# The lower half of the tokens in two parts of 256, and gathered expert steps moved between stages

## The chip, the cores and the metric

The kernel runs on one core of one Trainium2 chip. The metric is the device time of one execution in microseconds (us). Before the change three runs took 3245.26, 3264.1 and 3249.8 us, median 3249.8 us.

## What is computed

One layer of a decoder over 1024 tokens of width 1024 in float32:

```python
h = rms_norm(x, norm_mix_g); proj = h @ w_in          # 28 blocks of 128 columns and the gates
da_out = diff_attention(...)                           # 4 heads, causal, ALiBi
ml_out = rms_norm(o_gate * mlstm_chunkwise(...))       # 4 heads, state carried over the tokens
x = x + concat(da_out, ml_out) @ w_out
x = x + peer_ffn(rms_norm(x, norm_ffn_g), ...)         # expert retrieval
gate = sigmoid(rms_norm(x, norm_ple_g) @ w_ple_gate)
x = x + gate * (p @ w_ple_proj); out = rms_norm(x, final_norm_g)

def peer_ffn(x):                                       # per token
    q = x @ w_query                                    # 8 heads x 2 halves of 128
    sv, si = top_k(q . sub_keys, 16)                   # per half, of 128 keys
    top_s, eidx = top_k(all sums of two halves, 16)    # 16 of 16384 experts per head
    a = gelu(x . expert_u[eidx])
    return sum(softmax(top_s) * a * expert_v[eidx])    # 128 experts per token
```

## The kernel before

Tokens lie in eight tiles of 128. `front(part, ptk)` (L220) takes a part of `T` = 512 tokens (`NT` = 4 tiles) through the mixer, the output projection and the queries; it is called for part 0 (tiles 0 to 3) and part 1 (tiles 4 to 7). In it, `project` (L257) makes one of 29 projections: `weight` (L190) loads a block of 512 KB, ScalarE rounds it to `whi` (L195), VectorE takes the rest `wlo` (L196), and 24 matmuls (L143, eight 128-row pieces times three products) stream the part's tokens past it. Four heads follow each other, attention and mLSTM in each, with many short operations on 128 to 1024 columns; then eight blocks of `w_out` (L521), where the weights stream and the tokens stand in the array, and 16 blocks of `w_query` (L575), each followed on VectorE by five selecting operations per tile (L595 to L600).

The experts are computed in two ways. For tiles 0 to 3 (`NS` = 4), `topk2` (L607) settles the 128 experts of each token of two tiles in one call, and `sparse` (L704) then gathers their rows: one step is an indirect DMA of 128 rows of `expert_u` into a buffer `ru` and one of `expert_v` into `rv` (L700, 128 rows of 4 KB each, issued on GpSimd's queue), a dot product on VectorE (L716) and an accumulation on VectorE (L734). A tile has 128 such pairs, four tiles 512. Tiles 4 to 7 go densely: `dense_up` (L818) multiplies them with all of `expert_u` in 128 tables (`tlo` L754 once per table) and builds the gates, `dense_down` (L879) does the same with `expert_v` in 32 rounds of four tables. `tail` (L956) does the last gate, projection and norm for each tile.

What sets the order is a scheduler with priorities, and a generator that is advanced beside the main work. `pump(x)` (L212) adds x to a balance and takes one step of the generator per whole unit; the steps get a priority 800 places later (`LAG`), so they stand behind the main work near which they were taken. The rates:

```python
F_RATE = (2.4, 1.6, 2.0)     # per projection, per w_query block, per w_out block, in front(1) alone
UP_RATE = (1.5, 1.6, 56)     # per table of dense_up: 1.5 in the first 56, then 1.6
DOWN_RATE = 1.6              # per table of dense_down
TAIL_RATE = 8.0              # twice per tile in tail
pumped["gen"] = chain(lambda: topk2(0, ptk, [0]), lambda: topk2(0, ptk, [2]),
                      lambda: sparse(range(NS), rs))
```

A `topk2` call of two tiles is 14 generator steps, `sparse` over four tiles 528. The buffers for gathered rows are a ring of 4 per table in `front` and `dense_up`, 8 in `dense_down`, and 2 from round 27 of `dense_down` on (`FLUSH`) and in `tail`. Parts after the first load their tokens (L235, L251) on GpSimd's queue, the one that issues the gathers; SyncE's queue carries the weights.

Of the kernel before, what the change touches and what calls it, by code (L numbers as in the profile page):

```python
# [8 lines left out]
F32 = mybir.dt.float32  # L9
# [10 lines left out]
P = 128  # L20
# [49 lines left out]
TKEYS = [(0, q) for q in range(4)] + [(0, -1), (1, -1)] + [(1, q) for q in range(4)]  # L70
F_RATE = (2.4, 1.6, 2.0)
UP_RATE = (1.5, 1.6, 56)
DOWN_RATE = 1.6


@with_exitstack
def layer(ctx, tc, x, xT, pT, gcols, grows, win, convw, convb, gbias, lams, wout, wq, subk,
# [68 lines left out]
    def bcast_rows(pool, psum, cols, name):  # L146
        ps = psum.tile([P, NT, P], F32, name="tr")
        for i in range(NT):
            pe.matmul(ps[:, i, :], cols[:, i:i + 1].to_broadcast([P, P]), ident,
                      start=True, stop=True)  # L150
        r = pool.tile([P, T], F32, name=name)
        sc.activation(r, ps.rearrange("p a b -> p (a b)"), AF.Copy)
        return r
# [66 lines left out]
    def front(part, ptk):  # L220
        t0 = part * NT
        with ExitStack() as c1:
# [5 lines left out]
            with pool(f"pa{part}", bufs=1) as pa:  # L228
# [3 lines left out]
                for dc in range(DC):  # L232
                    if dc % 2 == 0:
                        x2t = pa.tile([P, 2, T], F32, name="p", bufs=3)
                        (gp if part else sy).dma_start(x2t, xT[part, :, dc:dc + 2, :])  # L235
# [94 lines left out]
                for h in range(H):  # L330
# [9 lines left out]
                    v.tensor_tensor(kT[:, part * T:(part + 1) * T], ps, rb, op=OP.mult)  # L340
                    ps = project(h * 7 + 2)
                    by_tile(vv[:, t0:t0 + NT, :], token_major(ps), lambda i: r1[:, i:i + 1])
                    if part < NPART - 1:
                        sy.dma_start(kt_s[h], kT[:, :T])
                        sy.dma_start(v_s[h], vv[:, :NT, :])

# [157 lines left out]
            with pool(f"pb{part}", bufs=1) as pb_:  # L504
# [13 lines left out]
                for blk in range(2):  # L518
                    pss = [sps.tile([P, 2, 512], F32, name="S") for _ in range(2)]
                    for q in range(4):  # L520
                        pump(F_RATE[2] * part)  # L521
                        hi, lo = weight(wp, wout[blk, q], [2, 512])
# [46 lines left out]
                for hc in range(2):  # L569
                    pump(F_RATE[1] * part)  # L570
                    pair.append((*weight(wp, wq[hc], [DC, P]), mmp.tile([P, T], F32, name="mm")))
                for cs in (slice(0, T // 2), slice(T // 2, T)):
                    for a in pair:
                        mm3s(query_terms(*a, cs), ("hl", "r"))
                for hc in range(2 * PH):  # L575
# [4 lines left out]
                    else:  # L580
                        pump(F_RATE[1] * part)
                        hi, lo = weight(wp, wq[hc], [DC, P])
# [24 lines left out]
    def topk2(part, pt_, tgs):  # L607
        sv, sfa = fcs["sv", part]
        t0 = part * NT
        if part in gsm:  # L610
# [9 lines left out]
    def topk2b(part, pt_, tgs):  # L620
        sv, sfa = fcs["sv", part]
        t0 = part * NT
        i0a, i1a = sel_i[part]
# [73 lines left out]
    def gather(k, tl, table, name):  # L697
        part, i = divmod(tl, NT)
        b = ring["pool"].tile([P, D], F32, name=name, bufs=ring["bufs"])
# [4 lines left out]
    def sparse(tiles, rs):  # L704
# [14 lines left out]
        def coef(n):  # L719
            tl, k0 = units[n]  # L720
            part, i = divmod(tl, NT)
            cf = rs.tile([P, K], F32, name="cf", bufs=2)
# [41 lines left out]
    def gate_blocks(gp_, pT_, pG):  # L764
# [5 lines left out]
        for n, tl in enumerate(DORD):  # L770
            part, i = divmod(tl, NT)
            fl = gp_.tile([P, 3, P], F32, name="fl", bufs=1)
# [45 lines left out]
    def dense_up(ptk):  # L818
        qh, ql = fcs["q"]
        chunks = [(qh, ql, 0, CH1)]  # L820
        with ExitStack() as c1:
# [134 lines left out]
    def tail(yac):  # L956
        with ExitStack() as c1:
# [5 lines left out]
            for tl in TORD:  # L963
                part, i = divmod(tl, NT)
                if tl < NS:
# [59 lines left out]
                for b in range(2):  # L1025
# [29 lines left out]
def layouts(i):  # L1055
# [27 lines left out]
    for h in range(H):  # L1083
# [57 lines left out]
```

## Time and profile before

| what | us |
|---|---|
| median of three runs | 3249.8 |
| the profiled execution, its own time | 3289.4 |
| its span, first to last instruction | 3287.6 |
| `front(0)` | 0 to 475 |
| `front(1)` | 475 to 1049 |
| `dense_up`, first to last matmul | 1049 to 1978 |
| `dense_down`, first to last matmul | 2000 to 2896 |
| from there to the end | 2896 to 3288 |

Busy shares over the span: TensorE matmul 82%, VectorE 81%, GpSimd 42%, ScalarE 32%. The engines are not busy in the same stages, so the shares are to be read by stage. PE is TensorE's matmuls, PEld its weight loads, DVE VectorE, ACT ScalarE, POOL GpSimd, SPq SyncE's DMA queue.

### The profile page before, as it was taken

What the parts mean: (1) busy time and instruction counts of PE and PEld (TensorE: products, weight loads), DVE (VectorE), ACT (ScalarE), POOL (GpSimd) and SP (SyncE); (2) the same over time, 40 slices, a digit from 0 to 9 for tenths busy, and PEclk for the clock granted to TensorE, in tenths of its full rate; (3) what the DMA queues carried; (4) which work ended last, traced back from release to release, by engine and by line L of the source; (5) the groups of instructions that cost most, each with busy time, mean ns of one, the idle gap of its engine ahead of it and who ended that gap; (6) DMA issues with size and microseconds to landing.
All of it is one profiled execution on the core that took longest, in us unless ns stands there. A gap on an engine that the chain in (4) does not pass through costs nothing.

```text
span 3287.6 us, 37409 instructions
## 1 busy us (share of the span) xinstructions
PE 2711.8 (82%) x12348; PEld 2143.1 (65%) x12348; DVE 2651.6 (81%) x5837; ACT 1046.9 (32%) x1755; POOL 1372.9 (42%) x1044
## 2 busy tenths in 40 slices
PE   8999889999989986999899996878888887827602
PEld 6777766576777765787787875666666666615401
DVE  5555697788899999887998987778888787998863
ACT  4445333344422323343344432222222222203200
POOL 0000000133332554655565674465555556674561
PEclk9999997799999996999999998989998988968856
DMA  3113431355674987999999999999999999997873
GB/s 137 65 63 107 143 120 38 119 188 183 237 260 151 350 311 272 380 377 371 366 412 367 413 408 370 351 371 352 359 360 362 339 383 371 389 336 271 265 258 119
DMA packets 326467, 911.85 MB, mean 277 GB/s; under 512 B 28480, under 2 KB 101056, under 8 KB 324224
## 3 DMA queue, kind: packets, MB, share of 16 engines
q0 software_dynamic: 149760, 545.33, 45.0%
q1 hardware_dynamic: 158080, 330.57, 27.9%
q10 hardware_dynamic: 18432, 33.56, 2.7%
q8 instruction: 97, 1.59, 0.2%
q14 instruction: 98, 0.80, 0.1%
HBM read 827.56 MB, written 81.79 MB: 277 GB/s over the span
## 4 chain that ended last, share of the span: by engine, by line
PE 37%; DMA 20%; DVE 18%; issue 16%; POOL 7%; ACT 2%; DVEq 0%; POOLq 0%; SPq 0%; ACTq 0%
PE mm L143 13%; PE A L143 9%; DMA raw<-in_vr 7%; DMA ru<-in_eu,eidx 5%; DMA rv<-in_ev,eidx 5%; DVE ya L734 4%; POOL rv L700 3%; POOL ru L700 3%; PE S L359 3%; DVE ru L716 3%; PE S L143 2%; DVE tlo L754 2%; PE tr L387 1%; PE pg L807 1%; PE pg L806 1%
## 5 line engine op out<-in xcount | busy, mean ns | idle before, releaser
L700 POOL DMA_INDIRECT ru<-in_eu,eidx x512 | 673.2, 1315 | 869.8 <-DVE ru L716 441.3
L700 POOL DMA_INDIRECT rv<-in_ev,eidx x512 | 690.6, 1349 | 507.9 <-DVE ya L734 304.0
L734 DVE SCALAR_TENSOR_TENSOR ya<-rv,cf,ya 128x1024 f32<-128x1024 f32 x512 | 657.0, 1283 | 101.7 <-DMA rv<-in_ev,eidx 78.6
L716 DVE SCALAR_TENSOR_TENSOR ru<-ru,sh 128x1024 f32<-128x1024 f32 x512 | 624.1, 1220 | 41.9 <-DMA ru<-in_eu,eidx 37.1
L753 ACT ACTIVATE thi<-raw 128x1024 fp32r<-128x1024 f32 x256 | 271.5, 1061 | 921.4 <-DMA raw<-in_vr 510.3
L143 PE MATMUL A<-ahi,thi 128*128 128x512 f32 x1024 | 408.0, 398 | 11.7 <-ACT ga L866 6.4
L754 DVE TENSOR_TENSOR tlo<-raw,thi 128x1024 fp32r<-128x1024 f32 x256 | 312.3, 1220 | 122.0 <-ACT thi L753 112.0
L143 PE MATMUL A<-alo,thi 128*128 128x512 f32 x1024 | 404.2, 395 | 0.0
L143 PE MATMUL keep<-thi,ph 128*128 128x512 f32 x1024 | 284.3, 424 | 144.6 <-ACT ph L916 75.7
L143 PEld LDWEIGHTS keep<-thi,ph 128*128 128x128 f32 x1024 | 207.4, 205 | 201.3 <-ACT ph L916 81.1
L143 PE MATMUL mm<-ahi,whi 128*128 128x512 f32 (+1 forms) x752 | 302.1, 406 | 17.4 <-ACT ahi L237 9.2
L143 PE MATMUL mm<-alo,whi 128*128 128x512 f32 (+1 forms) x752 | 292.5, 402 | 6.7 <-DVE alo L238 6.7
L143 PE MATMUL keep<-tlo,ph 128*128 128x512 f32 x1024 | 267.8, 406 | 20.4 <-DVE tlo L754 20.1
L143 PE MATMUL A<-ahi,tlo 128*128 128x512 f32 x1024 | 263.9, 401 | 23.9 <-DVE tlo L754 23.8
L143 PE MATMUL keep<-thi,pl 128*128 128x512 f32 x1024 | 256.9, 394 | 6.3 <-DVE pl L917 6.3
L143 PEld LDWEIGHTS keep<-tlo,ph 128*128 128x128 f32 x1024 | 203.6, 200 | 68.5 <-DVE tlo L754 23.7
L143 PEld LDWEIGHTS A<-ahi,tlo 128*128 128x128 f32 x1024 | 196.3, 193 | 70.5 <-DVE tlo L754 29.7
L143 PEld LDWEIGHTS A<-ahi,thi 128*128 128x128 f32 x1024 | 195.7, 191 | 57.9 <-ACT ga L866 12.1
L143 PEld LDWEIGHTS keep<-thi,pl 128*128 128x128 f32 x1024 | 195.0, 191 | 47.9 <-DVE pl L917 6.7
L143 PEld LDWEIGHTS A<-alo,thi 128*128 128x128 f32 x1024 | 195.6, 191 | 39.5
L143 PE MATMUL mm<-ahi,wlo 128*128 128x512 f32 (+1 forms) x752 | 196.0, 391 | 2.8 <-DVE wlo L196 2.8
L196 DVE TENSOR_TENSOR wlo<-wraw,whi 128x1024 fp32r<-128x1024 f32 x106 | 129.1, 1218 | 58.7 <-ACT whi L195 44.1
(436 smaller groups left out, 4149.2 us busy)
## 6 DMA issues: line engine op xcount, KB each, us to landing
raw<-in_ut SPq DMA_DIRECT2D x128, 512.0 KB, 7.0
raw<-in_vr SPq DMA_DIRECT2D x128, 512.0 KB, 7.8
ga_s<-ga ACTq DMA_DIRECT2D x128, 256.0 KB, 6.6
g_s<-st SPq DMA_DIRECT2D x16, 2048.0 KB, 10.4
gq<-g_s SPq DMA_DIRECT2D x32, 1024.0 KB, 9.9
aq<-ga_s SPq DMA_DIRECT2D x32, 1024.0 KB, 12.2
wraw<-in_win SPq DMA_DIRECT2D x58, 512.0 KB, 3.4
wraw<-in_wq SPq DMA_DIRECT2D x32, 512.0 KB, 4.1
```

Source lines behind the costliest of these rows:

```text
L143: pe.matmul(o, ll if p == "l" else lh, rl if p == "r" else rh, start=start and p == "h", stop=stop and n == last and p == names[-1])
L196: anchor(v.tensor_sub(lo.rearrange("p a b -> p (a b)"), raw, hi.rearrange("p a b -> p (a b)").bitcast(F32)))
L359: pe.matmul(sp_[:, n0:n1], qT[64 * c:64 * c + 64, i * P:(i + 1) * P], kT[64 * c:64 * c + 64, n0:n1], start=True, stop=False)
L387: pe.matmul(po, wT[:, kt, :], vv[:, kt, :], start=kt == 0, stop=kt == g)
L700: gp.indirect_dma_start(out=b, out_offset=None, in_=table, in_offset=bass.IndirectOffsetOnAxis(ap=eidx[part][:, i, k:k + 1], axis=0))
L716: behind(v.scalar_tensor_tensor(b, b, 1.0, st["h", tl], op0=OP.mult, op1=OP.mult, accum_out=st["d", n][:, j:j + 1]))
L734: op = v.scalar_tensor_tensor(ya, b, st["c", n][:, j:j + 1], ya, op0=OP.mult, op1=OP.add)
L753: sc.activation(hi, raw, AF.Copy)
L754: anchor(v.tensor_sub(lo, raw, hi.bitcast(F32)))
L806: pe.matmul(pg[:, b, :], o0[:, a, :, b], w0[:, a, :, b], start=True, stop=False)
L807: pe.matmul(pg[:, b, :], o0[:, a, :, b], w1[:, a, :, b], start=False, stop=True)
```

## The change

The parts become three, of 2, 2 and 4 tiles: `front(0)` has tokens 0 to 255, `front(1)` 256 to 511, `front(2)` 512 to 1023. All that had four tiles' width has the part's width now, each part loads and splits all weights for itself, and the keys and values of earlier parts are stored and read back. The generator starts after `front(0)` and takes tiles 0 and 1 first, then the selection of tiles 2 and 3, then these tiles.

```diff
+PARTS = ((0, 2), (2, 2), (4, 4))
+NPART = len(PARTS)
+LOC = {t0 + i: (n, i) for n, (t0, nt) in enumerate(PARTS) for i in range(nt)}
...
-F_RATE = (2.4, 1.6, 2.0)
+F_RATE = ((0.0, 0.0, 0.0), (1.0, 0.8, 1.0), (2.4, 1.6, 2.0))
 UP_RATE = (1.5, 1.6, 56)
-DOWN_RATE = 1.6
+DOWN_RATE = 1.85
...
     def front(part, ptk):
-        t0 = part * NT
+        t0, NT = PARTS[part]
+        T = NT * P
+        xT_ = xT[:, t0 * DC * P:(t0 + NT) * DC * P].rearrange("p (c t) -> p c t", c=DC)
+        f_rate = F_RATE[part]
...
                 def project(blk):
-                    pump(F_RATE[0] * part)
+                    pump(f_rate[0])
...
                     if part:
-                        sy.dma_start(kT[:, :T], kt_s[h])
-                        sy.dma_start(vv[:, :NT, :], v_s[h])
+                        sy.dma_start(kT[:, :t0 * P], kt_s[h, :, :t0 * P])
+                        sy.dma_start(vv[:, :t0, :], v_s[h, :, :t0, :])
...
-                    pss = [sps.tile([P, 2, 512], F32, name="S") for _ in range(2)]
+                    pss = [sps.tile([P, 2, 512], F32, name="S") for _ in range(NT // 2)]
...
-            late = chain(lambda: topk2(1, ptk, [0, 2]))
+            late = chain(lambda: topk2(2, ptk, [0, 2]))
...
-    pumped["gen"] = chain(lambda: topk2(0, ptk, [0]), lambda: topk2(0, ptk, [2]),
-                          lambda: sparse(range(NS), rs))
-    front(1, ptk)
+    pumped["gen"] = chain(lambda: topk2(0, ptk, [0]), lambda: sparse(range(2), rs), lambda: topk2(1, ptk, [0]),
+                          lambda: sparse(range(2, NS), rs))
+    for part in range(1, NPART):
+        front(part, ptk)
```

How the instructions stand on the engines, at three places. In all of them `ru,dots<-ru,sh` is the dot product with a gathered row, `ya<-rv,cf,ya` the accumulation.

VectorE, queries of the first part (`wlo` splits a weight block, `sv` are the selections from the scores `tr`). Before:

```order
697 L599 MAX sv_3226<-wk 128x8
698 L596 MAX_INDEX si<-sv_3226,tr 128x8
699 L600 MAX_INDEX si<-sv_3226,wk 128x8
700 L597 MATCH_REPLACE wk<-sv_3226,tr 128x128
...
711 L196 TENSOR_TENSOR wlo<-wraw,whi 128x1024
```

After:

```order
415 L199 TENSOR_TENSOR wlo<-wraw,whi 128x1024
416 L605 MAX sv_2396<-wk 128x8
417 L601 MAX sv_2396<-tr 128x8
418 L606 MAX_INDEX si<-sv_2396,wk 128x8
419 L602 MAX_INDEX si<-sv_2396,tr 128x8
420 L603 MATCH_REPLACE wk<-sv_2396,tr 128x128
421 L601 MAX sv_2396<-tr 128x8
...
426 L199 TENSOR_TENSOR wlo<-wraw,whi 128x1024
```

Between two weight blocks stand ten selecting operations now, where there were twenty; the split itself keeps its 1024 columns and is there for each part.

GpSimd's queue, where a later part's tokens are loaded (`p<-in_xT`, `p<-in_x`). Before, from the queue's start:

```order
6 L731 DMA ya<-x_s 128x1024
7 L712 DMA sh_6151<-h_s 128x1024
8 L235 DMA p<-in_xT 128x1024 x4
9 L251 DMA p<-in_x 128x1024 x4
10 L700 DMA ru<-in_eu,eidx_4456 128x1024 x4
11 L700 DMA rv<-in_ev,eidx_4456 128x1024
```

After, the loads of `front(2)`, with the buffer waits that the queue holds there shown in brackets:

```order
60 L706 DMA rv<-in_ev,eidx_3332 128x1024 [waits DMASW7_49,DVE_49]
61 L706 DMA ru<-in_eu,eidx_3332 128x1024 [waits DMASW0_49,DVE_49]
62 L241 DMA p<-in_xT 128x1024 [waits DMASW1_49,PE_49,Activation_49]
63 L241 DMA p<-in_xT 128x1024 [waits DMAHW4_49,DMAHW7_49,DMAHW0_49,DMASW2_49]
64 L241 DMA p<-in_xT 128x1024 [waits DMASW3_49]
65 L706 DMA rv<-in_ev,eidx_3332 128x1024 [waits DMASW4_49,DVE_49]
66 L241 DMA p<-in_xT 128x1024 [waits DMASW5_49,DMASW1_49,DVE_49]
```

The last part's tokens were loaded ahead of every gather; they stand behind some fifty gathers now, each of which waits for VectorE to free a buffer.

VectorE, the end of the gathered steps. Before, in the middle of `tail`, with the last tile's work (`al<-tr`) behind it:

```order
4428 L734 SCALAR_TENSOR_TENSOR ya<-rv,cf,ya 128x1024 x2
4429 L716 SCALAR_TENSOR_TENSOR ru,dots<-ru,sh_20479 128x1024 x2
4430 L724 TENSOR_TENSOR cf<-cf,gsm_4455 128x16
4431 L734 SCALAR_TENSOR_TENSOR ya<-rv,cf,ya 128x1024 x18
4432 L116 TENSOR_SCALAR r_m<-ss 128x1
```

After, where the first tile's work in `tail` begins:

```order
4405 L722 SCALAR_TENSOR_TENSOR ru,dots<-ru,sh_21509 128x1024
4406 L740 SCALAR_TENSOR_TENSOR ya<-rv,cf,ya 128x1024
4407 L730 TENSOR_TENSOR cf<-cf,gsm_17052 128x16
4408 L740 SCALAR_TENSOR_TENSOR ya<-rv,cf,ya 128x1024 x11
4409 L993 TENSOR_TENSOR al<-tr,ah 128x512 x2
```

The last dot product of the four tiles stood two rows ahead of the last tile's work and stands ahead of the first tile's now; five accumulations are left behind that row. Counted over VectorE's whole order, dots and accumulations by stage are: in the fronts 62 and 46 before, 31 and 15 (`front(1)`) and 93 and 93 (`front(2)`) now; in `dense_up` 198 and 198 before, 181 and 180 now; in `dense_down` 176 and 176 before, 188 and 189 now; between it and the first tile of `tail` 25 and 25 before, 19 and 30 now; behind that 51 and 67 before, 0 and 5 now.

## Rows read from the trace of the kernel before

**Rows 1.** The page: busy time by engine, the clock granted to TensorE in 40 slices of the span (tenths of full speed).
```profile
PE 2711.8 (82%) x12348; PEld 2143.1 (65%) x12348; DVE 2651.6 (81%) x5837; ACT 1046.9 (32%) x1755; POOL 1372.9 (42%) x1044
PEclk9999997799999996999999998989998988968856
```

**Rows 2.** Busy time in seven stretches that follow the stages: stretch and its length, then busy us of PE, PEld, DVE, ACT and POOL with the number of instructions, granted clock, busy share of the DMA engines, GB/s.
```profile
0.00:475.00 475.00, 435.95 (x2169) 340.82 (x2169) 296.84 (x1202) 211.17 (x481) 3.04 (x9) 0.96 0.29 101
475.00:1049.00 574.00, 540.82 (x2451) 392.03 (x2452) 491.06 (x1757) 222.99 (x485) 145.75 (x120) 0.90 0.50 170
1049.00:1978.00 929.00, 847.01 (x4115) 699.76 (x4113) 843.60 (x1405) 344.81 (x404) 533.62 (x387) 0.94 0.94 362
2000.00:2896.00 896.00, 752.23 (x3072) 606.04 (x3072) 720.14 (x923) 205.02 (x266) 481.79 (x362) 0.92 0.99 363
2896.00:2955.00 59.00, 2.71 (x10) 1.42 (x9) 57.79 (x76) 3.56 (x7) 44.34 (x37) 0.55 0.91 326
2955.00:3288.00 333.00, 133.05 (x535) 103.03 (x535) 231.22 (x464) 58.32 (x112) 149.06 (x119) 0.68 0.69 230
```

**Rows 3.** The same stretches, VectorE's work on `rv` alone (one instruction per accumulation).
```profile
475.00:1049.00 574.00, 58.90 (x46) 0.90 0.50 170
1049.00:1978.00 929.00, 248.17 (x194) 0.94 0.94 362
2000.00:2896.00 896.00, 225.30 (x176) 0.92 0.99 363
2896.00:2955.00 59.00, 29.02 (x23) 0.55 0.91 326
2955.00:3288.00 333.00, 89.73 (x70) 0.68 0.69 230
```

**Rows 4.** The chain of work that ended last, in order of time: start, length, what. From the fronts and `dense_up`: the first long run of projections; the same place in heads 2 and 3; output projection, transposes, the 256-column matmuls of the first queries, two later query blocks; a table of `dense_up`.
```profile
42.79 6.96 PE mm L143 x30
137.35 3.91 PE mm L143 x17
203.13 3.91 PE mm L143 x17
297.59 8.87 PE S L143 x38
349.41 5.55 PE tr L547 x24
361.45 10.13 PE mm L143 x86
440.38 5.51 PE mm L143 x24
446.87 5.50 PE mm L143 x24
1206.09 24.14 PE A L143 x104
```

**Rows 5.** Groups of instructions: line, engine, operation, out<-in, shapes, count; busy us, mean ns of one; idle time before them and what ended it.
```profile
L716 DVE SCALAR_TENSOR_TENSOR ru<-ru,sh 128x1024 f32<-128x1024 f32 x512 | 624.1, 1220 | 41.9 <-DMA ru<-in_eu,eidx 37.1 <-DMA sh<-h_s 4.2
L734 DVE SCALAR_TENSOR_TENSOR ya<-rv,cf,ya 128x1024 f32<-128x1024 f32 x512 | 657.0, 1283 | 101.7 <-DMA rv<-in_ev,eidx 78.6 <-issue 14.6 <-DMA ya<-x_s 7.9
L196 DVE TENSOR_TENSOR wlo<-wraw,whi 128x1024 fp32r<-128x1024 f32 x106 | 129.1, 1218 | 58.7 <-ACT whi L195 44.1 <-PE S L143 12.2 <-ACT sif L602 1.3
L143 PEld LDWEIGHTS mm<-ahi,whi 128*128 128x128 f32 x752 | 148.0, 197 | 43.6 <-ACT ahi L237 9.4 <-ACT whi L195 7.2 <-ACT t L267 1.8
L596 DVE FIND_INDEX8 si<-sv,tr 128x8 uint32<-128x128 f32 x128 | 37.2, 290 | 0.0
L404 DVE TENSOR_TENSOR cx<-mm,rb 128x512 f32<-128x512 f32 x16 | 10.9, 684 | 0.1
L977 DVE TENSOR_TENSOR pl__24722<-pf,ph__24721 128x256 fp32r<-128x256 f32 x1 | 0.4, 415 | 0.0
L665 DVE SCALAR_TENSOR_TENSOR tmp<-pos,dl 128x256 bf16<-128x256 bf16 x60 | 24.9, 415 | 0.1
L672 DVE TENSOR_TENSOR bb<-bb,tmp 128x256 bf16<-128x256 bf16 x60 | 17.0, 283 | 0.1
L670 DVE TENSOR_SCALAR tmp<-pos 128x256 bf16<-128x256 bf16 x60 | 13.0, 217 | 0.1
L649 DVE MAX8 ts<-wk 128x8 f32<-128x50 f32 x64 | 13.0, 205 | 0.0
```

**Rows 6.** The chain again, behind `dense_down`: gathers that it waits for one by one in `tail`, and the last tile.
```profile
2996.74 4.85 PE acc L143 x13
3208.62 10.54 DMA rv<-in_ev,eidx x3
3226.74 4.34 DMA rv<-in_ev,eidx
3232.72 4.37 DMA rv<-in_ev,eidx
3238.74 4.72 DMA rv<-in_ev,eidx
3270.49 5.45 PE acc L143 x24
```

More of the change, by code (lines that the diff above doesn't have):

```diff
@@ L146, in bcast_rows @@
     def bcast_rows(pool, psum, cols, name):
-        ps = psum.tile([P, NT, P], F32, name="tr")
-        for i in range(NT):
+        nt = cols.shape[-1]
+        ps = psum.tile([P, nt, P], F32, name="tr")
+        for i in range(nt):
             pe.matmul(ps[:, i, :], cols[:, i:i + 1].to_broadcast([P, P]), ident,
                       start=True, stop=True)
-        r = pool.tile([P, T], F32, name=name)
+        r = pool.tile([P, nt * P], F32, name=name)
         sc.activation(r, ps.rearrange("p a b -> p (a b)"), AF.Copy)
@@ L234, in front @@
                         x2t = pa.tile([P, 2, T], F32, name="p", bufs=3)
-                        (gp if part else sy).dma_start(x2t, xT[part, :, dc:dc + 2, :])
+                        (gp if part else sy).dma_start(x2t, xT_[:, dc:dc + 2, :])
                     xt = x2t[:, dc % 2, :]
@@ L336, in front @@
                     if part:
-                        sy.dma_start(kT[:, :T], kt_s[h])
-                        sy.dma_start(vv[:, :NT, :], v_s[h])
+                        sy.dma_start(kT[:, :t0 * P], kt_s[h, :, :t0 * P])
+                        sy.dma_start(vv[:, :t0, :], v_s[h, :, :t0, :])
                     ps = project(h * 7 + 1)
-                    v.tensor_tensor(kT[:, part * T:(part + 1) * T], ps, rb, op=OP.mult)
+                    v.tensor_tensor(kT[:, t0 * P:t0 * P + T], ps, rb, op=OP.mult)
                     ps = project(h * 7 + 2)
@@ L343, in front @@
                     if part < NPART - 1:
[L344 to L345 removed]
+                        sy.dma_start(kt_s[h, :, t0 * P:t0 * P + T], kT[:, t0 * P:t0 * P + T])
+                        sy.dma_start(v_s[h, :, t0:t0 + NT, :], vv[:, t0:t0 + NT, :])
                     osb = pa.tile([P, NT, P], F32, name="t2", bufs=T2)
@@ L518, in front @@
                 for blk in range(2):
-                    pss = [sps.tile([P, 2, 512], F32, name="S") for _ in range(2)]
+                    pss = [sps.tile([P, 2, 512], F32, name="S") for _ in range(NT // 2)]
                     for q in range(4):
-                        pump(F_RATE[2] * part)
+                        pump(f_rate[2])
                         hi, lo = weight(wp, wout[blk, q], [2, 512])
@@ L569, in front @@
                 for hc in range(2):
-                    pump(F_RATE[1] * part)
+                    pump(f_rate[1])
                     pair.append((*weight(wp, wq[hc], [DC, P]), mmp.tile([P, T], F32, name="mm")))
-                for cs in (slice(0, T // 2), slice(T // 2, T)):
+                for cs in (slice(0, T // 2), slice(T // 2, T)) if T > 256 else (slice(0, T),):
                     for a in pair:
@@ L580, in front @@
                     else:
-                        pump(F_RATE[1] * part)
+                        pump(f_rate[1])
                         hi, lo = weight(wp, wq[hc], [DC, P])
@@ L608, in topk2 @@
         sv, sfa = fcs["sv", part]
-        t0 = part * NT
+        t0, NT = PARTS[part]
         if part in gsm:
@@ L621, in topk2b @@
         sv, sfa = fcs["sv", part]
-        t0 = part * NT
+        t0, NT = PARTS[part]
         i0a, i1a = sel_i[part]
@@ L697, in gather @@
     def gather(k, tl, table, name):
-        part, i = divmod(tl, NT)
+        part, i = LOC[tl]
         b = ring["pool"].tile([P, D], F32, name=name, bufs=ring["bufs"])
@@ L720, in coef @@
             tl, k0 = units[n]
-            part, i = divmod(tl, NT)
+            part, i = LOC[tl]
             cf = rs.tile([P, K], F32, name="cf", bufs=2)
@@ L770, in gate_blocks @@
         for n, tl in enumerate(DORD):
-            part, i = divmod(tl, NT)
+            part, i = LOC[tl]
             fl = gp_.tile([P, 3, P], F32, name="fl", bufs=1)
@@ L963, in tail @@
             for tl in TORD:
-                part, i = divmod(tl, NT)
+                part, i = LOC[tl]
                 if tl < NS:
@@ L972, in tail @@
                 pf = ta.tile([P, 2, P], F32, name="pf", bufs=2)
-                sy.dma_start(pf, pT[part, :, :, i * P:(i + 1) * P])
+                sy.dma_start(pf, pT[tl])
                 ph = ta.tile([P, 2, P], F32R, name="ph_", bufs=2)
@@ L1094, in layouts @@
         x=x,
-        xT=x.reshape(NPART, T, DC, P).transpose(0, 3, 2, 1),
-        pT=a["p"][0, 0].reshape(NPART, T, 2, P).transpose(0, 3, 2, 1),
+        xT=np.concatenate([x[t0 * P:(t0 + nt) * P].reshape(nt * P, DC, P).transpose(2, 1, 0).reshape(P, -1)
+                           for t0, nt in PARTS], axis=1),
+        pT=a["p"][0, 0].reshape(S // P, P, 2, P).transpose(0, 3, 2, 1),
         gcols=gcols,
```

1 line of the change is left out of this document (removed).

## Prediction

> **What bounds the kernel now.** I read the page first, for the shares: matmul 82%, VectorE 81%, neither of them full [rows 1]. Shares over the whole span hide that each stage has its own limit, so the windows by stage come next [rows 2]. There the reader is to see four regimes. In `front(0)` TensorE is busy 436 of 475 us, VectorE 297: TensorE sets the pace. In `front(1)` both are high, 541 and 491 of 574. In `dense_up` and `dense_down` the DMA engines are busy 0.94 and 0.99 of the time, at 362 to 363 GB/s, with VectorE at 844 of 929 and 720 of 896 beside them. Behind `dense_down` nothing is full: in the last 333 us TensorE works 133, VectorE 231, the DMA share is 0.69.
>
> What fills that last stretch is seen in the count of accumulations by stage [rows 3]: 23 in the 59 us after the last dense matmul and 70 in the last 333. And the chain of waits shows what they cost there: three gathers in 10.54 us in a row, then one at 3226.74, one at 3232.72, one at 3238.74 [rows 6], 6.0 us apart. With a ring of two buffers the steps run one behind another, and the last tile can't start before the last of them. So the tail is bound by gathers in their latency, the dense stages by gathers in their bytes, and the first front by matmuls while VectorE and the DMA engines (share 0.29) have room.
>
> **The change part by part.** Counts by stage are those of VectorE's order in the part on the change; I price each stage in the profiled execution.
>
> *Tail.* Removed are 51 dots and 67 accumulations behind the first tile's start; 5 accumulations stay. The stretch before it keeps its length, since 49 row operations stand there for 50: 59 us. From `dense_down`'s end to the second gate run of the first tile, which ends at 2996.74 + 4.85 = 3001.6 [rows 6], pass 105.6 us; the six dots and five accumulations in between go, and weights no longer land beside gathers, so I take 95. The other seven tiles then cost TensorE's own time: 48 + 12 matmuls of 512 columns at 24.14/104 = 0.232 us [rows 4], 13.9 us, and with eight transposes 14.7; seven are 103. The last tile's end behind its last matmul is 3287.6 - 3275.9 = 11.7 us [rows 6], kept. 95 + 103 + 12 = 210 us instead of 392: **-182**, I write -180. Bounds: -195 with no wait for weights, and -85 if the seven tiles ran at half clock, 97 us more; the mean clock there is 0.68 now [rows 2].
>
> *`dense_down`.* 188.5 pairs of rows instead of 176. A pair is 2 x 128 x 4 KB = 1.05 MB, at 363 GB/s [rows 2] 2.89 us: 12.5 pairs are **+36**. By VectorE, 1.22 + 1.28 us a pair [rows 5], it would be +31.
>
> *`dense_up`.* 180.5 pairs instead of 198 in the order: by bytes -17 x 2.89 = -49. But one selection of 256 tokens comes in: 15 rounds of two operations like L665, three like L672 and one like L670, 28 us, and 16 scans of five like L649 at 0.205, 16 us [rows 5], together 45; 17 pairs less give VectorE back 43. VectorE was busy 844 of 929 [rows 2], so it can't let the stage shrink far, and while the selection of tiles 2 and 3 runs no rows can be gathered at all. Between -49 and +3 I take **-20**, nearer the middle.
>
> *Fronts.* Added are 53 weight blocks (29 + 8 + 16): 53 loads of 512 KB on SyncE's queue, at a DMA share of 0.29, 53 roundings on ScalarE (211 of 475 us busy), and 53 x 1.22 = 65 us of splits on VectorE [rows 2, 5]. Matmuls on 256 columns cost 10.13/86 = 0.118 us, on 512 5.51/24 = 0.230 [rows 4]: two halves are 0.236, so TensorE pays nearly nothing. VectorE's wide operations do pay: 0.684 us on 512 columns and 0.415 on 256 [rows 5], 0.15 more for two.
>
> A head takes 203.13 - 137.35 = 65.8 us now [rows 4]: seven projections, 38.6, and 27 of other matmuls. On 256 tokens the projections are 7 x 24 x 0.118 = 19.8; the other 27 I split by key width into 11 and 16. TensorE's share of a head is then 31 in the first part and 36 in the second. VectorE's: (297 less some 100 for queries and 50 around them)/4 = 36 now, 8.5 of it splits; halved but for the splits and fixed starts, 24. In the first part TensorE leads and I add 4 us for the chain of short operations that no longer has 512-column matmuls to hide it: 35. In `front(1)` VectorE carries beside that one selection (45) and, up to the queries, 25 dots and 8 accumulations (41): 86/4 = 21 more, 45 a head, and VectorE leads.
>
> `front(0)`: 36 to the first steady projections (42.79 now [rows 4], with twice the tokens to load), 4 x 35 = 140, output projection 52 -> 27 (its columns stay 512, the count halves), transposes 12 -> 8 [rows 4]. A query block takes 6.5 us now [rows 4]; TensorE's side falls to 24 x 0.118 and its scores, 3.1, but VectorE has the split, 1.22, and ten selecting operations of up to 0.29 [rows 5]. Twenty and a split fill the 6.5 now, which makes 0.26 for one: 3.86, and 62 for 16 blocks. With 8 to the end, 281 us. `front(1)`: a shorter start, 22, 4 x 45 = 180, 39 for output projection, transposes and end, 62 + 16 for queries with 6 dots and 7 accumulations beside them: 319. `front(2)` against `front(1)` before: two selections leave (90), 31 dots and 47 accumulations come (98): +8, in which the wait of its token loads behind the gathers on GpSimd's queue is a few us of start. Sum 281 + 319 - 475 + 8 = **+133**. Bounds: +60 if heads run at TensorE's 31 and 36 and the rest hides; +261 by heads of 50 and 62 (below).
>
> Sum: -180 + 36 - 20 + 133 = **-31** on the profiled execution's 3289.4, 3258.4. The median of the runs is 3249.8, 0.988 of the profiled time; so the forecast is **3219 us**, 0.9% below.
>
> [...] PEld shows 197 ns per weight load of the projections [rows 5], yet the 86 narrow matmuls, each with a load of its own, passed in 10.13 us, 0.118 each [rows 4]: the loads ran beside each other's matmuls. [...]
>
> **The rivals.**
>
> *Heads stay long (slower).* The mechanism is the in-order VectorE queue in a head of 256 tokens: a split stands behind short attention and mLSTM operations and behind a dot product that waits for its gather, TensorE runs out of split weights (two buffers), and the chain does not halve with the tokens. Place: the heads of `front(0)` and `front(1)`. Price: heads of 50 and 62 us instead of 35 and 45 are +128, so 3345. It decides from 4 us more per head, where the forecast's gain is gone. For it: VectorE is at 0.86 in `front(1)` already [rows 2]. Against it: in `front(0)` TensorE is idle 39 of 475 us only, so now the chain is mostly hidden. A lower clock belongs here: where TensorE works 133 of 333 us, the granted clock is 0.68 [rows 2].
>
> *Fronts hide everything (faster still).* Heads at 31 and 36, the added VectorE work in its free 38%: fronts +60, 3147. For it: `front(0)` leaves VectorE 178 us free [rows 2]. Against it: `front(1)` gets 86 us more.
>
> *The dense stages take the gain back.* The bytes moved forward into them cost, none is saved in `dense_up` (+3), and the tail's clock and weights give only -150: 133 + 36 + 3 - 150 = +22, 3272.
>
> *Weight loads set the pace.* If the 45 x 24 narrow matmuls of both parts came 0.197 us apart, a load's duration [rows 5], instead of 0.118: 2160 x 0.079 = +171, about 3388. The row of 86 speaks against it. [...]
>
> **How the numbers follow.** A measurement of this kernel can tell about 0.5%, 16 us, from no change: 3234 and 3266 are the lines. The forecast has 0.50; its own range, 3180 to 3270, puts 0.34 below 3234, 0.12 within, 0.04 above. Heads stay long 0.20, all slower. Fronts hide everything 0.19, all faster. Dense stages take it back 0.08: 0.05 within (its 3272 is near the line), 0.03 above. Weight loads 0.03, slower. Faster 0.53, same 0.17, slower 0.30. That the change doesn't do what it says is excluded by the order. For 8 in 10 the range runs from 3145, which takes in the hidden fronts, to 3320, which takes in heads of some 48 and 58 us.
>
> **What would show it.** In the changed profile: the stretch behind the last dense matmul near 210 us, with no gather in its chain after the first tile (right), or over 260 (wrong). `dense_down` near 932 us, its DMA share still 0.99. Both lower fronts near 281 and 319 us, the second with VectorE over 0.8 busy; the narrow matmuls at 0.118. `front(2)` near 582. If the two lower fronts together pass 635 us, the forecast of faster is wrong, and heads of over 39 and 49 us each will be where; if they stay below 540, it is too careful.

## The result, and the profile after the change

The changed kernel takes 3306.1 us, median of four runs (3287.6 to 3312.9); beside it the kernel before takes 3253.5. The ratio is 1.0139, 95% interval 1.0104 to 1.0174: **slower by 1.4%, 53 us**, where 0.9% faster was forecast. The profiled execution took 3287.6 us, the shortest of its four, with a span of 3285.8. The page, as in [rows 1]:

```profile
PE 2754.0 (84%) x13388; PEld 2234.6 (68%) x13388; DVE 2738.1 (83%) x6069; ACT 1121.1 (34%) x1908; POOL 1371.8 (42%) x1050
PEclk8899998899898989979999999988999899898679
```

The stretches that answer to [rows 2] are below, with the same columns: `front(0)`, `front(1)`, `front(2)`, `dense_up`, the gap, `dense_down`, the stretch up to the first tile of `tail`, the rest; the last row is the queries of `front(2)`.

```profile
0.00:281.00 281.00, 245.17 (x1580) 218.68 (x1580) 185.31 (x707) 134.62 (x312) 3.08 (x9) 0.90 0.43 143
281.00:598.00 317.00, 250.89 (x1628) 214.73 (x1628) 276.97 (x1036) 142.81 (x315) 61.63 (x55) 0.89 0.58 198
598.00:1195.00 597.00, 533.56 (x2457) 396.60 (x2457) 517.39 (x1442) 229.99 (x497) 249.93 (x197) 0.90 0.68 234
1195.00:2123.00 928.00, 843.80 (x4108) 696.60 (x4108) 837.11 (x1545) 345.53 (x403) 476.31 (x351) 0.95 0.89 341
2123.00:2157.00 34.00, 0.18 (x1) 0.18 (x2) 17.73 (x24) 2.22 (x5) 17.53 (x15) 0.55 1.05 390
2157.00:3076.00 919.00, 755.32 (x3072) 608.28 (x3072) 750.62 (x960) 204.77 (x265) 513.97 (x387) 0.91 0.99 364
3076.00:3135.00 59.00, 2.57 (x9) 1.42 (x9) 57.80 (x72) 6.84 (x12) 41.85 (x35) 0.52 0.94 346
3135.00:3286.00 151.00, 122.55 (x535) 98.09 (x535) 95.13 (x291) 54.29 (x105) 7.53 (x5) 0.90 0.28 99
1070.00:1191.00 121.00, 102.74 (x482) 82.21 (x480) 117.61 (x524) 27.08 (x45) 40.85 (x30) 0.93 0.60 200
```

VectorE's accumulations by stage, against [rows 3]:

```profile
281.00:598.00 317.00, 17.71 (x14) 0.89 0.58 198
598.00:1195.00 597.00, 120.46 (x95) 0.90 0.68 234
1195.00:2123.00 928.00, 223.23 (x174) 0.95 0.89 341
2157.00:3076.00 919.00, 243.42 (x189) 0.91 0.99 364
3076.00:3135.00 59.00, 34.08 (x27) 0.52 0.94 346
3135.00:3286.00 151.00, 11.00 (x9) 0.90 0.28 99
```

The chain of waits, against [rows 4] and [rows 6]: a long run of narrow projections in `front(0)` and in `front(1)`, the tokens that `front(2)` starts with, the last gathers, the first and the last run of the tail's matmuls.

```profile
105.10 8.08 PE mm L145 x52
340.31 8.37 PE mm L145 x71
...
596.48 7.07 DMA p<-in_xT
608.51 6.30 DMA p<-in_x
...
3143.96 13.57 DMA rv<-in_ev,eidx x2
3167.11 9.59 PE acc L145 x39
...
3268.90 5.45 PE acc L145 x24
```

The reader is to see that the mechanism is there: no gather in the chain after the first tile, the last 151 us at a granted clock of 0.90 where 333 us ran at 0.68, and lower fronts of 281 and 317 us. What is not as forecast is the upper front and `dense_up`. Some cautions on these rows. The window of `front(1)` ends at 598 us, but its last query is copied at 586.0 (that of `front(0)` at 279.4): the 12 us between belong to `front(2)`, which waits for its tokens there. In the kernel before, `front(0)`'s last query is copied at 465.1, so that the window of [rows 2] that opens at 475 misses the first 10 us of `front(1)`. And the 52 matmuls in the first row of the chain stood 0.213 us apart up to 109.5 us, at a granted clock of 0.52, and 0.118 behind it, at 1.00; over the whole of `front(0)` the clock was 0.90, where before it was 0.97.

The kernel before was profiled again, and this second trace is the better base: its execution (span 3249.7) lies at the median, where the first (3287.6) lies 36 us above it. Its stages, same columns:

```profile
0.00:466.00 466.00, 433.15 (x2168) 338.47 (x2168) 288.63 (x1160) 206.42 (x475) 3.04 (x9) 0.97 0.30 101
466.00:1019.00 553.00, 510.54 (x2457) 376.45 (x2457) 498.98 (x1804) 227.33 (x493) 146.51 (x121) 0.95 0.53 178
1019.00:1942.00 923.00, 842.99 (x4108) 696.18 (x4107) 837.45 (x1394) 344.20 (x401) 530.12 (x385) 0.95 0.94 362
1971.00:2858.00 887.00, 754.48 (x3070) 608.00 (x3071) 717.80 (x921) 204.27 (x265) 482.14 (x362) 0.92 1.00 366
2858.00:3250.00 392.00, 136.43 (x548) 103.97 (x546) 289.40 (x540) 61.84 (x119) 191.26 (x155) 0.67 0.73 245
...
475.00:560.00 85.00, 80.98 (x372) 55.02 (x373) 76.91 (x392) 39.00 (x78) 2.64 (x5) 0.98 0.26 86
```

By these windows `front(1)` takes 553 us here and took 574 in [rows 2]; from the last query of the part ahead to its own last query it is 553 here and 583 in the first trace. The last row is where most of it lies; in the first trace the same stretch reads

```profile
475.00:560.00 85.00, 81.41 (x283) 49.75 (x284) 61.33 (x324) 29.91 (x59) 2.64 (x5) 0.74 0.21 72
```

283 matmuls at a granted clock of 0.74, against 372 at 0.98: one program, one place, two clocks. The first 7 of the "77" in [rows 1] covers this stretch.

| stretch, us | before, 1st trace | before, 2nd | after | forecast for after |
|---|---|---|---|---|
| to `dense_up`'s first matmul | 1049.5 | 1018.9 | 1194.9 | 1182 |
| `dense_up` | 922.6 | 923.5 | 927.3 | 903 |
| gap | 29.1 | 28.4 | 34.6 | 29 |
| `dense_down` | 894.6 | 887.5 | 917.2 | 932 |
| behind it | 391.8 | 391.4 | 211.8 | 210 |

The rows are set by the first and last matmul of each stage, so single us differ from the windows.

### The profile page after: what moved, and what is told of

The parts are those of the page before. It is cut to its first block, busy times and chain, and to the rows that moved or that the text cites. A ratio compares the mean times of both kernels' runs of the same rounds, so it can differ in the third digit from the quotient of the medians.

```text
span 3285.8 us, 40243 instructions
## 1 busy us (share of the span) xinstructions
PE 2754.0 (84%) x13388; PEld 2234.6 (68%) x13388; DVE 2738.1 (83%) x6069; ACT 1121.1 (34%) x1908; POOL 1371.8 (42%) x1050
## 4 chain that ended last, share of the span: by engine, by line
PE 39%; DVE 22%; DMA 20%; issue 13%; ACT 3%; POOL 3%; DVEq 0%; SPq 0%; ACTq 0%; POOLq 0%
PE A L145 10%; PE mm L145 10%; DVE ya L740 6%; DMA aq<-ga_s 5%; DMA raw<-in_vr 5%; DMA rv<-in_ev,eidx 3%; DVE ru L722 3%; PE acc L145 3%; DVE tlo L760 3%; PE S L365 2%; PE keep L145 2%; PE S L145 2%; DMA ru<-in_eu,eidx 2%; POOL ru L706 2%; POOL rv L706 1%
## 5 line engine op out<-in xcount | busy, mean ns | idle before, releaser
L706 POOL DMA_INDIRECT ru<-in_eu,eidx x512 | 655.9, 1281 | 909.2 <-DVE ru L722 406.4
L706 POOL DMA_INDIRECT rv<-in_ev,eidx x512 | 703.5, 1374 | 549.5 <-DVE ya L740 302.9
L759 ACT ACTIVATE thi<-raw 128x1024 fp32r<-128x1024 f32 x256 | 271.8, 1062 | 927.3 <-DMA raw<-in_vr 523.3
L145 PE MATMUL mm<-ahi,whi 128*128 128x256 f32 (+1 forms) x1096 | 346.9, 339 | 45.8 <-ACT ahi L243 28.2
L145 PE MATMUL mm<-alo,whi 128*128 128x256 f32 (+1 forms) x1096 | 334.7, 334 | 3.7 <-DVE alo L244 3.7
L145 PEld LDWEIGHTS mm<-ahi,whi 128*128 128x128 f32 x1096 | 222.1, 203 | 60.8 <-ACT ahi L243 29.1
L198 ACT ACTIVATE whi<-wraw 128x1024 fp32r<-128x1024 f32 x159 | 168.1, 1058 | 236.7 <-PE mm L145 99.5
L145 PE MATMUL mm<-ahi,wlo 128*128 128x256 f32 (+1 forms) x1096 | 216.2, 330 | 18.4 <-DVE wlo L199 17.7
L145 PEld LDWEIGHTS mm<-alo,whi 128*128 128x128 f32 x1096 | 217.3, 202 | 18.3 <-DVE alo L244 5.2
```

Of the source, the lines that this page charges most:

```text
L145: pe.matmul(o, ll if p == "l" else lh, rl if p == "r" else rh, start=start and p == "h", stop=stop and n == last and p == names[-1])
L198: sc.activation(hi.rearrange("p a b -> p (a b)"), raw, AF.Copy)
L706: gp.indirect_dma_start(out=b, out_offset=None, in_=table, in_offset=bass.IndirectOffsetOnAxis(ap=eidx[part][:, i, k:k + 1], axis=0))
L759: sc.activation(hi, raw, AF.Copy)
```

## Experiments

**1. Both kernels again, unchanged.**

> The kernel before, unchanged, for a second trace. Theory A (the stage sums of the forecast were right in the two profiled executions, and the execution of before that they were made against was itself long): span near 3250 us, some 36 us below the first trace's 3287.6, with the fronts again at 475 and 574 within 5 us and the loss found in dense_up, dense_down or behind them. Theory B (the trace of before was typical and the timed runs differ from profiled ones): span near 3288 again with the same stage lengths.

> The changed kernel, unchanged, for a second trace and a second ratio: 1.010 to 1.018 against before. Theory A: a span of 3300 to 3312, longer than the first trace's 3285.8, fronts again 281, 317 and 597 within 5 us, the tail 210; what is longer lies in the DMA-bound stages. Rival C (the narrow fronts vary): the fronts together are 15 us or more longer than the 1195 of the first trace.

Measured: 3254.3 us, ratio 1.0014 [0.9983, 1.0045], and 3301.2 us, 1.0142 [1.0113, 1.0170]. The slowdown stands. The second trace of the change has its stages within 10 us of the first (fronts 1204.9, `dense_up` 929.7, `dense_down` 914, tail 211.9). Seven traces of programs with the same `front(0)` and `front(1)` as before have their first up-projection matmul at 1018.9, 1024.1, 1024.3, 1027.7, 1043.6, 1049.5 and 1052.8 us; the granted clock at 475 to 560 us is 0.98, 0.89, 0.89, 0.85, 0.72, 0.74 and 0.68 in that order. Five of them belong to kernels that ran several times. There the two short ones (1018.9 and 1024.3) have spans at the median of their kernels, and the three long ones lie 16 to 36 us above it. So the 574 us on which `front(2)` was sized are a low-clock reading that an execution at the median does not have. From last query to last query the seven take 553 to 587 us, and the second trace of before is the shortest of them.

**2. The pace alone: before, with the new pace of `dense_down`.**

```diff
-DOWN_RATE = 1.6
+DOWN_RATE = 1.85
```

> The kernel before with DOWN_RATE 1.85 and nothing else. Steps that leave the tail: 28 dots and 28 accumulations; they go to dense_down (+24 pairs) and the stretch behind it (+4). Theory of the forecast (a pair costs 2.89 us in dense_down by its bytes, about 4.8 us in the tail by latency): dense_down +70 us, tail -120 to -140, sum -50 to -70, ratio 0.98 to 0.985. Rival (dense_down is so full that every pair pushed into it also delays tables): ratio 1.0 or above.

Measured: 3206.9 us, ratio 0.9848 [0.9821, 0.9876]. Its trace in `dense_down` and behind:

```profile
2001.00:2940.00 939.00, 762.69 (x3070) 613.14 (x3071) 775.26 (x991) 206.99 (x266) 530.67 (x408) 0.90 1.01 372
2940.00:3232.00 292.00, 134.80 (x547) 105.02 (x546) 232.06 (x470) 61.89 (x118) 134.52 (x109) 0.73 0.72 245
```

24 pairs more cost `dense_down` 52 us (2.2 each); the 24 that are gone behind it give back 99 (some 4 each). This version beats both kernels: one line of the diff alone gains more than was forecast for the whole.

**3. The split alone: the change, with the old pace.**

```diff
-DOWN_RATE = 1.85
+DOWN_RATE = 1.6
```

> The changed kernel with DOWN_RATE back at 1.6: three parts, old pace. 18 pairs leave dense_down against the change, 17 dots and 28 accumulations come back to the tail. If the split alone is the loss: fronts 1195 as in the change; dense_down 919 - 18 x 2.89 = 867; tail 210 + 17 to 28 steps of 5 to 6 us = 300 to 340; sum about 3310 to 3350, slower than the change by 0 to 1.5%. If the higher pace is the loss instead, it is faster than the change.

Measured: 3308.8 us, ratio 1.0174 [1.0128, 1.0220]. Fronts 1196.7, tail 257. The split by itself costs 1.7%. What the new pace gains on top of it, 0.3 points, is not clear of the noise (the two intervals overlap). By the traces the split alone had taken 33 of the 92 accumulations that stood behind `dense_down`.

**4. `front(1)` without gathered steps.**

```diff
-F_RATE = ((0.0, 0.0, 0.0), (1.0, 0.8, 1.0), (2.4, 1.6, 2.0))
+F_RATE = ((0.0, 0.0, 0.0), (0.0, 0.0, 0.0), (2.4, 1.6, 2.0))
```

> The changed kernel with the rates of front(1) at 0: neither selection nor gathers run beside the second part; the selection of tiles 0 and 1 falls into front(2). Theory V (VectorE leads front(1), 86 us of selection and rows are in its way): from front(1)'s first token rounding to its last query copy, 303 us in the change, 260 to 275. Rival P (TensorE and the chain of short operations lead): 295 or more. front(2) gets 45 us of selection for 27 pairs: 590 to 610. About 41 pairs come back to the tail, 210 -> 320 to 340; in all slower than the change, 3360 to 3400.

Measured: 3369.0 us, 1.0338 [1.0286, 1.0389]. From the first rounded tokens (ScalarE's first `ahi` of the part) to the last query `front(1)` takes 275 us for 303; VectorE has some 75 us less to do there. The steps come back behind `dense_down`, 353 us. The start of `front(2)` is read from it below.

**5. `front(2)`'s tokens on SyncE's queue.**

```diff
-                        (gp if part else sy).dma_start(x2t, xT_[:, dc:dc + 2, :])
+                        (gp if part == 1 else sy).dma_start(x2t, xT_[:, dc:dc + 2, :])
...
-                    (gp if part else sy).dma_start(xk, x[(t0 + i) * P:(t0 + i + 1) * P, :])
+                    (gp if part == 1 else sy).dma_start(xk, x[(t0 + i) * P:(t0 + i + 1) * P, :])
```

> The changed kernel with the token loads of front(2) on SyncE's queue instead of GpSimd's. If the loads are late because they stand behind gathers on GpSimd's queue: from the last query copy of front(1) to the first token rounding of front(2), 17 us in the change, 2 to 6 us, and the kernel 10 to 15 us faster than the change (ratio to before 1.009 to 1.012). Rival (they wait for their buffers, whichever queue): the gap stays at 14 to 18 us, no change.

Measured: 3299.2 us, 1.0120 [1.0074, 1.0166]. TensorE's waits at the start of the last part (what for, us in total, times, longest): in the second trace of before, the change, experiment 4 and this one.

```profile
PE mm L143 <- DVE alo L238: 7.0, 1, 7.0
PE mm L143 <- ACT ahi L237: 2.6, 2, 1.8
```
```profile
PE mm L145 <- ACT ahi L243: 17.1, 1, 17.1
```
```profile
PE mm L145 <- ACT ahi L243: 3.9, 2, 3.4
PE mm L145 <- DVE alo L244: 2.2, 1, 2.2
```
```profile
PE mm L145 <- ACT ahi L243: 16.9, 2, 13.2
```

The wait is for rounded tokens. It is short where no gathers run ahead, and hardly shorter where the tokens have left GpSimd's queue. When the first of these loads were issued says why: the second trace of before, experiment 4, the change, and last this experiment, with the five loads of weights that stand ahead of them on SyncE's queue.

```profile
366.06 0.53 POOL L235 DMA_DIRECT2D p<-in_xT  x1
```
```profile
494.59 0.53 POOL L241 DMA_DIRECT2D p<-in_xT  x1 [208.52 <-PE mm L145]
```
```profile
596.48 1.68 POOL L241 DMA_DIRECT2D p<-in_xT  x3
```
```profile
573.82 15.85 SPq L195 DMA_DIRECT2D wraw<-in_win  x5
589.76 1.69 SPq L241 DMA_DIRECT2D p<-in_xT  x3
```

The last query of the part ahead is copied at 464.5, 554.2, 586.0 and 582.3 us. So the loads were issued 98 and 60 us ahead of it in the first two, and 10 and 7 us behind it in the others; the first took 5.0 us to land in experiment 4, 7.1 in the change and 6.2 here. The wait is a late issue. That the steps beside `front(1)` cause it is shown by experiment 4, which takes the selection out with the gathers. This experiment does not test GpSimd's queue by itself, because it moved the loads from behind the gathers to behind weight loads that held SyncE's queue for 16 us; what those waited for stays open.

**6. `front(1)` without its weight splits.** VectorE's 53 splits are left out there and `hi` stands in for `lo`, so that this kernel drops the low part of these weights.

```diff
+        if bare["on"]:
+            anchor(sc.activation(hi.rearrange("p a b -> p (a b)"), raw, AF.Copy))
+            return hi, hi
...
+        bare["on"] = part == 1
```

> The changed kernel without the splits of the 53 weight blocks in front(1): the rounded weights stand for the rest, which leaves the low part of the weights out there. 53 x 1.22 = 65 us of VectorE's 277 go. Theory V (VectorE leads front(1)): its 303 us fall by 40 to 55. Rival P: by 0 to 15. Four dots and three accumulations more run in front(1) in this order, 9 us.

Measured: 3264.5 us, 1.0009 [0.9986, 1.0031]. `front(1)` takes 280 us for 303: 65 us less of splits, with 11 us of rows more in their place, gave 23, between the two expectations. `front(2)` is 7 us shorter, `dense_up` 5 longer. The two profiled executions lie 26 us apart, the medians 37 to 42; the rest is in no trace. VectorE is a part of what paces `front(1)`, not all.

**7. Fewer rows in `dense_up`** (before; two runs).

```diff
-UP_RATE = (1.5, 1.6, 56)
+UP_RATE = (1.1, 1.25, 56)
```

> The kernel before with UP_RATE (1.1, 1.25): dense_up holds 178 to 179 pairs instead of 198 and still two selections. It prices a pair there without the third selection. If a pair costs 2.5 us (VectorE) to 2.9 us (bytes): dense_up 923 -> 866 to 875. Then the change's dense_up, 17 pairs less and 928, has paid some 45 us for the selection. If dense_up stays at 915 or more, pairs are free there and the selection cost nothing. About 47 pairs go to the tail, 390 -> 530 to 560 us: slower in all, some 3350.

> The kernel before with no rows paced into dense_up (UP_RATE 0): 27 pairs of rows are left there of 198, 250 to 266 more stand in the tail, so the whole is far slower (about 3254 + 220 x 3.2 = 3950 or more); what is read is dense_up's length between the first and the last matmul of the up-projection, 919 to 923 us before. Theory (TensorE with its waits for gates and splits sets dense_up; it is busy 845 of 925 us there; a pair costs little): 885 to 910. Rival 1 (a straight line through the run with 19.5 pairs fewer, 0.65 us a pair): 924 - 171 x 0.65 = 813, which is below TensorE's own busy time, so 850 at least. Rival 2 (the prediction's term, bytes or VectorE's time): 700 to 850, with TensorE over 0.98 busy at the upper end.

The second has (0.0, 0.0, 56). Measured 3369.3 and 3994.8 us in single runs; `dense_up` 911 and 845 us, for 923.5 in the second trace of before. The window of the second:

```profile
1028.00:1873.00 845.00, 831.45 (x4107) 694.05 (x4107) 455.96 (x883) 342.71 (x391) 73.33 (x56) 0.99 0.54 191
```

171 pairs less save 78 us, 0.46 each, and TensorE is then busy 831 of 845 us. The theory's 885 was too high. The 845 lies in the second rival's range, but at its end, where TensorE is the limit; the first version, 0.65 us a pair, shows that the prediction's 2.89 is far too much. On the mean of the stage a pair costs a sixth of its bytes' time, though the DMA share reads 0.94. Experiment 9 shows that this mean hides two parts.

**8. More pace** (before). Three versions: `DOWN_RATE` 2.1; `DOWN_RATE` 2.0, `FLUSH` 116, `NPRE` 2; `DOWN_RATE` 1.95 with these two and `F_RATE` (2.8, 1.6, 2.4).

> The kernel before with DOWN_RATE 2.1 (pairs of rows by VectorE's order: dense_down 224, behind the first tile of the tail 0 dots and 11 accumulations; with 1.85 they were 200 and 23/39). Theory (each pair taken out of the tail gives back its latency, about 3.2 us, and costs its bytes in dense_down, 2.2 us): dense_down 939 + 24 x 2.2 = 992, stretch behind it 292 -> 212 to 225, net -15 to -28 on pace_only: ratio to the kernel before 0.976 to 0.982. Rival (dense_down is saturated, a further pair costs 2.9 us or more there): dense_down 1009 or more, net 0 or worse: 0.985 to 0.990.

> The kernel before with DOWN_RATE 2.0, the ring of eight kept for two rounds more (FLUSH 116 for 108), and two of the tail's weights loaded ahead for four. Pairs: dense_down 214, between it and the first tile 38/48, behind that 0/6. Theory (latency of a ring of two is what a late pair costs): dense_down 939 + 14 x 2.2 = 970, stretch behind it 225 to 240, ratio 0.974 to 0.982. Rival (the tail's weights, not yet loaded, take the place of the gathers): stretch 255 or more, ratio 0.985 or above.

> The kernel before with F_RATE (2.8, 1.6, 2.4), DOWN_RATE 1.95, FLUSH 116, two weights ahead: front(1) 75/59 pairs for 62/46, dense_up 199/197, dense_down 210/212, between 28/44, behind 0/0. Theory (front(1) takes 13 pairs for about 1 us each, the tail's floor is the 210 us of the changed kernel): front(1) 551 to 574 + 13, dense_down 966, stretch behind it 212 to 230; ratio 0.972 to 0.980. Rival (VectorE sets front(1)'s length: 13 pairs cost 2.5 us each): front(1) +33, ratio 0.980 to 0.990.

Measured: 3214.7 us, 0.9857 [0.9832, 0.9883]; 3215.3, 0.9860 [0.9831, 0.9888]; 3240.2, 0.9934 [0.9903, 0.9966]. In all three the ratio missed the theory and came out at the rival's or above it. In the first `dense_down` is 997 us, nearer the theory's 992 than the rival's 1009: some 23 further pairs cost 58 us (2.5 each). What failed is what they gave back, 53 us for 67 to 80:

```profile
1995.00:2992.00 997.00, 761.65 (x3072) 613.86 (x3072) 830.33 (x1062) 207.50 (x268) 584.27 (x454) 0.88 1.01 375
2991.00:3230.00 239.00, 125.99 (x550) 99.88 (x549) 181.62 (x401) 61.31 (x116) 75.49 (x63) 0.76 0.56 199
```

In the second `dense_down` is 970 us, as the theory has it, but the stretch behind it 272, not 225 to 240. In the third `front(1)` came to 592 us, 40 more than in the second trace of before, and 35 of these lie in its queries:

```profile
922.00:1058.00 136.00, 105.44 (x484) 84.26 (x483) 130.91 (x542) 27.11 (x45) 52.41 (x41) 0.89 0.65 220
```

**9. Fewer rows in `front(2)`** (the change).

```diff
-F_RATE = (..., (2.4, 1.6, 2.0))
+F_RATE = (..., (1.4, 0.4, 1.0))
```

> The change with F_RATE[2] = (1.4, 0.4, 1.0): front(2) gets 59 pairs of rows where it had 93, about as many as front(1) of the kernel before, and no selection; the later stages get the rest (tail 45/61). What is read is front(2)'s length, from 597 us. Theory of the prediction (VectorE's time sets it, 2.5 us a pair): 34 pairs less are -85 at most, -45 to -70 expected: 527 to 552. Rival (VectorE's rows hide in front(2); the 40 to 50 us over front(1) before come from the late start and the first head): 0 to -20: 577 to 597. The whole is slower than the change in either case, by the tail (+120 to +150).

Measured: 3368.1 us, a single run; `front(2)` is 31 us shorter for 34 pairs less, between the expectations. It falls in two parts. The queries take 101 us, not 121:

```profile
1067.00:1168.00 101.00, 96.50 (x480) 78.73 (x480) 98.47 (x509) 27.46 (x46) 13.27 (x8) 0.98 0.35 114
```

By VectorE's time on rows, the queries of the last part took 101 us with 11.8 us of rows (this run), 101 with 18.5 (second trace of before: 8.55 + 9.92), 111 with 24.1 (experiment 6: 11.27 + 12.83), 121 with 34.3 (the change: 16.33 + 17.93), 136 with 48.1 (the third of experiment 8: 23.13 + 24.96). From 12 to 18 us of rows the time does not move: TensorE is busy 96.5 of the 101 us and VectorE 98 and 100. Beyond that VectorE stays at 0.96 busy or more, TensorE falls to 0.90, 0.85 and 0.78, and each us of rows is a us or more of time.

Ahead of the queries it is another matter: from the first rounded tokens 466 us with 199 us of rows in the change, 456 with 135 here, 450 with 116 and two selections in the second trace of before. There neither the rows that came nor the selections that left moved much. The length goes with the clock that TensorE was granted (the change, this run, the second trace of before, the first version of experiment 8):

```profile
604.00:1070.00 466.00, 429.55 (x1968) 313.31 (x1969) 393.31 (x888) 200.80 (x449) 207.25 (x166) 0.90 0.71 242
```
```profile
611.00:1067.00 456.00, 422.68 (x1971) 305.87 (x1972) 337.80 (x811) 199.62 (x447) 143.26 (x117) 0.92 0.57 194
```
```profile
467.00:917.00 450.00, 413.07 (x1975) 296.88 (x1976) 396.85 (x1304) 198.62 (x448) 122.98 (x105) 0.94 0.54 181
```
```profile
466.00:941.00 475.00, 440.47 (x1969) 312.10 (x1970) 396.55 (x1300) 198.16 (x446) 122.18 (x104) 0.88 0.51 171
```

The same matmuls keep TensorE busy 16 us longer in the change than in the second trace of before, and another 11 us longer in a kernel that has before's `front(1)` unchanged. Over all fifteen traces this stretch runs from 450 us at 0.94 to 484 at 0.86, with 114 to 197 us of rows in no order.

The run also has a `dense_up` of 875 us, for 928 in the change, with about as many pairs (some 171 for 175). The selection of tiles 2 and 3 has moved behind the stage. But 45 of the 53 us lie in the first 960 of its 3072 up-projection matmuls (the change, this run, the second version of experiment 7):

```profile
1195.00:1509.00 314.00, 262.48 (x1220) 210.28 (x1221) 304.99 (x759) 102.96 (x122) 168.58 (x122) 0.91 0.86 320
```
```profile
1169.00:1438.00 269.00, 254.85 (x1223) 209.86 (x1223) 254.76 (x704) 104.08 (x122) 104.80 (x79) 0.99 0.79 296
```
```profile
1028.00:1302.00 274.00, 260.45 (x1221) 212.43 (x1221) 225.38 (x676) 103.48 (x122) 66.93 (x51) 0.96 0.68 248
```

The selections for the dense tiles fall there, VectorE is 0.97 busy in the change, and its rows take 151, 95 and 52 us: the 56 us between the first two cost 45, the 43 between the other two nothing. Behind the 960 the change takes 614 us with 287 of rows and the last version 572 with 11, so that there 276 us of rows and the selection cost 42 together.

## Why the prediction failed

*Tail, -180:* right, 391.4 to 211.8. *`dense_down`, +36:* measured +30; a pair costs 2.2 to 2.4 us, not 2.89. *Lower fronts, 281 + 319 - 475 = +125:* right in sum, +122 from last query to last query (279.4 + 306.6 against 464.5). In part this is luck: the heads of `front(0)` took 39 us for 35 and those of `front(1)` a mean of 43 for 45, and what stands around the heads of `front(0)` took 122 us for 141. The rival of long heads had the sign, not the cause: the two parts pass 598 us, below its mark of 635. *Narrow matmuls:* 8.37/71 = 0.118 us each, though `front(1)` and `front(0)` issue a load with every one, and a load took 0.188 us in that row: the loads ran beside the matmuls, and the rival of weight loads is false.

**The step that failed first is the upper front, "`front(2)` against `front(1)` before: +8".** From the last query of the part ahead to its own last query, `front(2)` takes 605.3 us and `front(1)` before 553.4 (second trace): +52. Of it 15 are the wait for tokens (17.6 us from the last query to the first rounding, for 2.3; by TensorE's own idle time 17.1 for 9.6, since before waits another 7.0 us behind its first rounding), 17 lie between there and the queries, 20 in the queries. The prediction balanced VectorE's times over the whole part, 98 us of rows in against 90 us of selections out. But the selections had stood beside heads that TensorE paces (ahead of the queries 413 of 450 us busy), and gave nothing back; six more pairs stand beside queries that VectorE paces (118 of 121 us busy), and those cost their full time (experiments 8 and 9). The wait was priced at "a few us". The 17 are TensorE's clock, 0.90 for 0.94, and are not shown to belong to the change: before's own `front(1)` has taken 450 to 484 us there, the change 467 and 474 in its two traces. And the base was the low-clock reading of 574, 583 from last query to last query, which alone hides 30 of the 52. Against the median of the seven traces of before, 565, the change's two traces (605 and 612) are +41 and +47, where +8 was forecast.

**The second is `dense_up`, -20:** +4 measured. The prediction took the middle between bytes and VectorE's time for the whole stage. By the traces the pairs that left are all gone from behind the first 960 matmuls, where TensorE paces and rows cost little (287 us of rows there for 336 before; in the first 960 it is 151 for 146). The selection came in at the same place: VectorE is busy 532 us there in both kernels, and the stretch takes 614 us for 609. What the selection costs by itself was not tested.

**The third is the scaling by 0.988.** It took the profiled execution's excess out of the kernel after as well. Of the 38 us between the two spans of before, 31 lie in the fronts and 7 in `dense_down`. So this is the low base again, seen from the sum, and no further loss: the table below, against the second trace, holds it in the row of the fronts.

| term (us, against the second trace) | forecast | measured |
|---|---|---|
| fronts | +133 | +176 |
| `dense_up` | -20 | +4 |
| gap | 0 | +6 |
| `dense_down` | +36 | +30 |
| tail | -180 | -180 |
| sum | -31 | +36 |

The profiled executions differ by 36 us, the medians by 53 and 47 in two comparisons: the change's profiled execution was its shortest. What sets its longer ones apart was not traced, beyond the second trace (span 3295.6), whose fronts took 10 us more.

What decided faster or slower: the split costs the fronts 176 us against the second trace and would pay only through the tail, where the pace alone takes 99 of the same 180 for 52 us of `dense_down` (experiment 2).

## What to carry to other kernels

A stage that is to be the base of a difference wants its granted clock read first: a stretch at 0.74 with the same code at 0.98 in another execution is no base, and scaling the sum does not mend it. Where seven traces of one stretch differ by 34 us, one of them does not price a term of 8. Balance an engine's work within each sub-stage where that engine leads, never over a stage: ahead of the queries 59 us less of VectorE's work, beside a TensorE that was busy 0.92 of the time, gave nothing back (397 us in 450 in the second trace of before, 338 in 456 in experiment 9). And price each part of a change by itself; here one number of the pacing table, without the rest, gained more than the forecast for all of it.

## What the runs showed of the hardware

After an idle of 6.7 to 7.0 us at the start of `front(1)`, TensorE's granted clock in the next stretch of 85 us came out at 0.98, 0.89, 0.74, 0.72 and 0.68 in five executions of the same code there (before twice, experiment 2 and two of experiment 8); from the shortest to the longest, the stage behind it began 34 us later. VectorE's row work cost nothing or its full time by place: none from 12 to 18 us beside the queries and a us or more for each us above that, 45 us for 56 in the first third of `dense_up`, and at most 42 for 276 in the rest. And a DMA share of 0.94 in `dense_up` did not mean that bytes set the time: with a share of 0.54 the stage was 8% shorter.
